# Down projection by block products over pairs of chunks, and products accumulated onto one another in PSUM

## The chip, the cores and the metric

The kernel runs on one core of a Trainium2 chip. The metric is device time in microseconds (us) of one execution; smaller is better. Engines are named as the profile names them: PE is TensorE (matmul), DVE is VectorE, ACT is ScalarE, POOL is GpSimd, SP is SyncE, which issues most loads and stores.

## What is computed

One layer of a hybrid decoder on 1024 tokens of width 1024: a token mixer (linear attention and sliding-window attention) and a gated MLP with a causal convolution of three taps. The change touches the MLP alone:

```
h2 = rms_norm(x, ffn_norm)
u = causal_dwconv(h2 @ w_up, conv_w, conv_b)     # w_up: 1024 x 5632
a, bval = jnp.split(u, 2, axis=-1)               # 2 x 2816
return x + (jax.nn.silu(a) * bval) @ w_down      # w_down: 2816 x 1024
```

All of it is float32. A float32 operand is split into a high half (`CAST` on ACT) and a low half (a subtraction, `split`), and a product is three matmul passes: high by high, high by low, low by high (`PASSES`).

## The kernel before

The hidden width of 2816 is cut into 22 chunks of 128 (`NCH`). A chunk takes 128 columns of the a side and 128 of the b side of `w_up`, for all 1024 tokens in two halves of 512.

**Up projection.** In chunks 1 to 20 the 2 by 2 blocks (side by token half, and 1024 rows of `w_up` in two halves) are made with seven block products instead of eight, the Strassen-Winograd scheme. `up_operand` builds the sums S1 to S4 on POOL, casts the high half on ACT and subtracts the low half on POOL; the token side (T1 to T4) is built once, in `norm2_sums`. Each of P1 to P7 is 12 matmuls of 128x512 into a PSUM bank of its own (`bank`, a pool of eight), and `post` adds the products up in SBUF: P1 and P5 are copied by ACT, DVE adds the other five, and from chunk 2 on POOL makes two more additions. `conv` is one ACT instruction (last tap and bias) and two DVE instructions (`tap`) on each half; `conv_edge` carries two columns from one token half to the other. `silu` is on ACT, `glu` multiplies a and b on DVE and splits the result into `g` (high half ACT, low half DVE). Chunks 0 and 21 use eight plain products (R1, R2, X1 to X4).

**Down projection.** For each chunk, 16 times (8 token tiles by 2 column halves), `down` makes three matmuls into a bank and DVE adds the bank to the SBUF accumulator `acc` (five of chunk 20's go over ACT and POOL, `VIA_POOL`). The down work of chunk c stands between the products of chunk c+1, as `SEQ` says: so many after each product.

**What sets the order.** All work is put into a list of events with a time each (`at_us`), sorted, and issued in that order; a scheduler of the framework then moves single instructions within each engine's queue. An engine's queue is executed in order. Operands are prepared four products ahead (`LAG`); the split operands lie in slots of SBUF (`SLOTS`: seven for the up side, two for the down side).

Of the kernel before, what the change touches and what calls it, by code (L numbers as in the profile page):

```python
# [35 lines left out]
def hymba_layer_kernel(ctx, tc, x, mix_norm, w_in, w_alpha2, b_alpha, gla_norm,  # L36
# [31 lines left out]
    SLOTS = {"w": tuple(i % 9 for i in range(48)) + (9, 3, 4, 5, 6, 7, 8, 0),  # L68
             "u": (1, 2, 3, 4, 5, 6, 7), "d": (8, 0)}
    used = {"w": 0, "u": 0, "d": 0}  # L70

    def w_tile(name, kind="w"):
        slots = SLOTS[kind]
        slot = slots[used[kind] % len(slots)]
        used[kind] += 1
        p = w_late["pool"] if slot == 9 else w_keep
        return p.tile([P, 2, 512], F32R, tag=f"w{slot}", name=name, bufs=1)
# [631 lines left out]
    def b_operand(name, k, r):  # L709
# [9 lines left out]
            "X3": ("A21", "T1"), "X4": ("A22", "B22")}  # L719

    def product(ch, name, part=None):
        an, bn = PROD[name]
# [1 line left out]
        first, last = name not in ("X2", "X4"), name not in ("X1", "X3")
        key = {"X1": "X2", "X3": "X4"}.get(name, name)
        if first and not part:
            psb[key, ch] = bank(f"{key}_{ch}")
        pb = psb[key, ch]
# [38 lines left out]
    done = {ch: set() for ch in range(NCH)}

    def post(ch, name):
        eng = dve if ch < 2 else pool  # L770

        def early(n):
            if ch:
                return half_tile(f"{n}_{ch}")
            if n in ("P1c", "R1c"):
                psb["early", n] = w_tile(f"{n}_0", "d").bitcast(F32)
            return psb["early", {"c11": "P1c", "c21": "R1c"}.get(n, n)][:, int(n[0] == "c")]

        if name in ("X1", "X3"):
            return  # L780
        pb = psb.pop((name, ch))
        if name in ("P1", "P5", "R1"):
            p = psb[name.lower(), ch] = early(f"{name}c")
            act.copy(p, pb)
        elif name == "P6":
            u2 = psb["u2", ch] = half_tile(f"u2_{ch}")
            dve.tensor_add(u2, psb["p1", ch], pb)
        elif name == "P2":
            c11 = psb["p1", ch] if "P6" in done[ch] else early("c11")
            dve.tensor_add(c11, psb["p1", ch], pb)  # L790
            conv(ch, 0, 0, c11, None)
# [255 lines left out]
```

## Time and profile before

| | us |
|---|---|
| median of 3 runs (1126.53 to 1126.87) | 1126.79 |
| the profiled execution, its own time | 1127.78 |
| its span, first to last instruction | 1125.9 |
| PE busy in the span | 1103.6 |
| POOL busy | 617.4 |
| DVE busy | 809.0 |
| ACT busy | 443.7 |

Busy time is the time in which an engine has an instruction in execution. DVE and POOL instructions that stand in each other's way show as longer instructions, not as idle time. A "releaser" is the engine and line whose result ended a wait. Matmuls overlap: one takes 0.40 us from start to end, and twelve in a row 2.80 us. MLP times in the trace: chunk 1 begins at 451 us, chunk 2 at 483 us, and the last chunks end with the span.

### The profile page before, as it was taken

Reading aid. Unit: us, or ns where it says so; the run is one execution under the profiler, and the core shown is the slowest. Engines: PE = TensorE matmul, PEld = TensorE weight load, DVE = VectorE, ACT = ScalarE, POOL = GpSimd, SP = SyncE. Lnnn points to the kernel's source line nnn. Section 1 sums busy time; section 2 is a strip of 40 time slices with the busy share of each in tenths; the row PEclk is TensorE's granted clock in tenths of the full one; section 3 lists DMA queues with packets and bytes.
Section 4 is the critical chain, followed back from the end, with each engine's and each line's share of the span. In section 5 each row is a group of like instructions: output and inputs, shape, how many; then the busy total and the mean of one; then the engine's idle time right before and its main releaser. Section 6 shows DMA issues by size and latency. Waiting matters only on the chain.

```text
span 1125.9 us, 14419 instructions
## 1 busy us (share of the span) xinstructions
PE 1103.6 (98%) x5276; PEld 887.4 (79%) x5276; DVE 809.0 (72%) x1479; ACT 443.7 (39%) x889; POOL 617.4 (55%) x491
## 2 busy tenths in 40 slices
PE   7999999999999999989999999999999999999997
PEld 5897778777888877778888888888888888888885
DVE  6646557766231489998878777777988788787777
ACT  5326655434240354433333433343434343333322
POOL 5356323334450356867657667776666666667402
PEclk9999999999999999999999999999999999999999
DMA  6124123002034101211111111111111211111103
GB/s 207 49 74 125 41 57 75 20 1 77 1 102 160 57 1 38 60 54 56 56 56 56 57 38 38 57 56 56 47 48 56 57 57 57 56 32 45 56 1 149
DMA packets 67344, 67.16 MB, mean 60 GB/s; under 512 B 4616, under 2 KB 51913, under 8 KB 67274
## 3 DMA queue, kind: packets, MB, share of 16 engines
q1 hardware_dynamic: 63432, 61.53, 17.7%
q10 hardware_dynamic: 3842, 4.73, 1.8%
q8 instruction: 41, 0.67, 0.2%
q14 instruction: 29, 0.24, 0.1%
HBM read 57.33 MB, written 4.19 MB: 55 GB/s over the span
## 4 chain that ended last, share of the span: by engine, by line
PE 87%; DVE 7%; POOL 3%; ACT 1%; issue 1%; DMA 1%; SPq 0%; POOLq 0%; DVEq 0%; ACTq 0%
PE P L734 33%; PE dn L852 20%; PE do L283 5%; PE dg L283 4%; PE dr L283 4%; PE dv L283 4%; PE dq L283 3%; PE dk L283 2%; DVE cu L755 2%; PE pv L444 1%; PE dq L633 1%; PE ppt L432 1%; PE X L734 1%; PE go L547 1%; PE go L543 1%
## 5 line engine op out<-in xcount | busy, mean ns | idle before, releaser
L852 PE MATMUL dn<-dnw,g 128*128 128x512 f32 x1056 | 270.1, 399 | 6.4 <-DVE g L836 3.0
L852 PEld LDWEIGHTS dn<-dnw,g 128*128 128x128 f32 x1056 | 199.9, 190 | 56.4 <-DVE g L836 3.4
L861 DVE TENSOR_TENSOR acc<-acc,dn 128x512 f32<-128x512 f32 x347 | 227.8, 681 | 2.7 <-PE dn L852 1.2
L283 PE MATMUL do<-wow,big 128*128 128x512 f32 x384 | 91.5, 397 | 0.0
L283 PEld LDWEIGHTS do<-wow,big 128*128 128x128 f32 x384 | 71.5, 188 | 16.8
L755 DVE SCALAR_TENSOR_TENSOR cu<-u,cc,cu 128x511 f32<-128x511 f32 (+2 forms) x120 | 80.4, 695 | 0.0
L84 POOL TENSOR_TENSOR dnw<-dn,dnw 128x512 fp32r<-128x512 f32 x44 | 57.5, 1307 | 28.9 <-ACT dnw L81 28.9
L84 POOL TENSOR_TENSOR A22w<-up,A22w 128x512 fp32r<-128x512 f32 x22 | 29.5, 1342 | 69.8 <-ACT A22w L81 65.7
L755 DVE SCALAR_TENSOR_TENSOR cu<-P1c,cc,cu 128x511 f32<-128x511 f32 (+1 forms) x46 | 51.1, 1110 | 21.5 <-ACT cu L747 21.3
L734 PE MATMUL P<-big,A11w 128*128 128x512 f32 x264 | 65.6, 396 | 0.9 <-ACT big L244 0.9
L421 POOL TENSOR_TENSOR pr<-pr,sm 128x1024 f32<-128x1024 f32 (+1 forms) x16 | 28.6, 1787 | 66.9 <-DVE sm L419 51.2
L734 PE MATMUL P<-big,A12w 128*128 128x512 f32 x264 | 65.3, 396 | 0.0
L734 PE MATMUL P<-big,S1w 128*128 128x512 f32 x240 | 62.4, 395 | 0.0
L734 PEld LDWEIGHTS P<-big,A11w 128*128 128x128 f32 x264 | 49.4, 188 | 13.1 <-ACT big L244 1.1
L734 PE MATMUL P<-ex,S2w 128*128 128x512 f32 x240 | 59.2, 395 | 0.0
L734 PE MATMUL P<-ex,S3w 128*128 128x512 f32 x240 | 59.2, 395 | 0.0
L734 PE MATMUL P<-ex,A22w 128*128 128x512 f32 x240 | 59.1, 395 | 0.0
L734 PE MATMUL P<-big,S4w 128*128 128x512 f32 x240 | 59.1, 395 | 0.0
L734 PEld LDWEIGHTS P<-big,A12w 128*128 128x128 f32 x264 | 49.6, 188 | 11.8
L836 DVE TENSOR_TENSOR g<-cu,g 128x512 fp32r<-128x512 f32 (+1 forms) x46 | 47.2, 1031 | 15.4 <-ACT g L835 15.4
L765 ACT ACTIVATE cu<-cu 128x512 f32<-128x512 f32 x44 | 27.9, 633 | 73.6 <-DVE cu L755 73.5
L734 PEld LDWEIGHTS P<-big,S1w 128*128 128x128 f32 x240 | 45.4, 189 | 11.0
(403 smaller groups left out, 2318.4 us busy)
## 6 DMA issues: line engine op xcount, KB each, us to landing
up<-in_w_up_dram SPq DMA_DIRECT2D x44, 512.0 KB, 3.8
dn<-in_w_down_dram SPq DMA_DIRECT2D x22, 512.0 KB, 4.2
acc<-in_x_dram SPq DMA_DIRECT2D x8, 512.0 KB, 7.9
out_dram<-acc SPq DMA_DIRECT2D x16, 256.0 KB, 2.1
xt<-in_x_dram SPq DMA_DIRECT2D x7, 512.0 KB, 4.4
qraw<-in_w_in_dram SPq DMA_DIRECT2D x4, 512.0 KB, 7.6
vraw<-in_w_in_dram SPq DMA_DIRECT2D x4, 512.0 KB, 3.5
qt<-qt ACTq DMA_DIRECT2D x16, 128.0 KB, 2.3
```

What stands on the lines that cost most here:

```text
L84: (eng or pool).tensor_sub(lo, src, hi.bitcast(F32))
L283: pe.matmul(pb[:, :n], lhsT=big[:, t, k, ra, :], rhs=ws[k][:, rb, :n], start=(k == 0 and i == 0), stop=(k == KD - 1 and i == 2))
L421: pool.tensor_tensor(pr[:, :, s0:], pr[:, :, s0:], den[:, hs].rearrange("p (j o) -> p j o", o=1).broadcast_to((P, 4, n)), ALU.mult)
L432: pe.transpose(pb[:, j * P:(j + 1) * P], pr[:, j, b * P:(b + 1) * P], ident)
L444: pe.matmul(pb[g * 64:(g + 1) * 64, :], lhsT=vv[:, t - 1 + b, g * 64:(g + 1) * 64], rhs=pts[t, g][:, b, :], start=(b == b0), stop=(b == 1))
L543: pe.matmul(pb[:, h * P:(h + 1) * P], lhsT=a[:, lo, pr * P:(pr + 1) * P], rhs=v[:, h * P:(h + 1) * P], start=(h == 0), stop=False)
L734: pe.matmul(pb[:, ts.start * P:ts.stop * P], lhsT=w[:, ra, k, :], rhs=b_operand(bn, k, rb)[:, ts], start=(first and i == 0), stop=(last an ...
L755: dve.scalar_tensor_tensor(dst, src, w, dst, op0=ALU.mult, op1=ALU.add)
L765: act.activation(u, u, AF.Silu)
L836: dve.tensor_sub(gt[:, 1], ub, gt[:, 0].bitcast(F32))
L852: pe.matmul(pb, lhsT=g[:, ra, (t % 4) * P:(t % 4 + 1) * P], rhs=w[:, rb, :], start=(i == 0), stop=(i == 2))
L861: dve.tensor_add(acc[:, cs], acc[:, cs], pb)
```

## The change

**Down projection.** Chunks 0 to 19 are taken in ten pairs. The 2 by 2 blocks (chunk of the pair by token half, and chunk by column half) are made with seven block products. A unit `down_pair(p, k, j)` is product k of pair p for two token tiles: six matmuls (2 tiles by 3 passes) into a pair of banks, one bank for each tile, and one DVE addition of 128x2x512 from both banks to `acc`. A product is two units, so a pair has 14 units. `down_w` makes the weight side (four POOL combinations in a pair, seven splits on ACT and POOL), `down_g` the token side (four DVE combinations, seven splits on ACT and DVE). One unit stands after each up product, from the second product of chunk 2 to the first of chunk 20, then two. Chunks 20 and 21 stay plain (`down_row`).

**Accumulation in PSUM.** P6, P7 and P4 are accumulated onto P1's bank and P3 onto P5's (`ONTO`), after the earlier content has been read; the down products likewise (`ONTO_DOWN`): P6, P7 and P4 onto P1's banks, P3 onto P5's. `post` so loses two DVE additions of a chunk and both POOL additions; the taps of P4 read PSUM. P2 now stands ahead of P6 in `SEQ`.

**Storage.** PSUM is four single banks for the up products and two pairs of banks for the down units (`open_banks`). The up operands have three slots in turn and are prepared two products ahead instead of four; the combinations are written over the loaded weights. The down operands have two slots on each side, and the rows of `w_down` two. `VIA_POOL` goes; `silu` of a chunk is one instruction over 1024 columns.

```diff
+NPAIR = NCH // 2 - 1
-VIA_POOL = ((NCH - 2, 3, 1), (NCH - 2, 4, 1), (NCH - 2, 5, 1), (NCH - 2, 6, 1), (NCH - 2, 7, 1))
...
+    def open_banks():
+        ps_first.close()
+        ps["b"] = ctx.enter_context(tc.tile_pool(name="psu", bufs=4, space=PSUM))
+        ps["d"] = ctx.enter_context(tc.tile_pool(name="psd", bufs=2, space=PSUM))
...
         if name == "S2":
-            s1 = combo("S1", "tensor_add", a21, a22)
-            src = combo("S2", "tensor_sub", s1, a11)
+            s1 = psb["S1", ch] = fin["ff"].tile([P, 4, P], F32, tag="s", name=f"S1_{ch}", bufs=1)
+            pool.tensor_add(s1, a21, a22)
+            pool.tensor_sub(a21, a11, a21)
+            pool.tensor_sub(a11, s1, a11)
...
+            slot = 1 + turn[0] % 3
...
+    ONTO = {"P6": "P1", "P7": "P1", "P4": "P1", "P3": "P5"}
...
     def post(ch, name):
...
+        if name == "P1":
+            ca = psb["ca", ch] = wide_tile(f"ca{ch}", "ca")
+            act.copy(ca[:, 0:512], pb)
+        elif name == "P2":
+            ca = psb["ca", ch]
+            dve.tensor_add(ca[:, 0:512], ca[:, 0:512], pb)
+            ua = psb["ua", ch] = wide_tile(f"ua{ch}", "ua")
+            conv(ch, 0, ua, ca, 0, 512, True)
         elif name == "P6":
+            act.copy(psb["ca", ch][:, 512:], pb)
+        elif name == "P5":
+            p5 = psb["p5", ch] = half_tile(f"p5_{ch}")
+            act.copy(p5, pb)
         elif name == "P7":
+            p5 = psb["p5", ch]
+            dve.tensor_add(p5, p5, pb)
+            ub = psb["c", ch, 1] = half_tile(f"ub1_{ch}")
+            conv(ch, 1, ub, p5, 0, 512, True)
+        elif name == "P3":
+            ca, ua = psb["ca", ch], psb["ua", ch]
+            dve.tensor_add(ca[:, 512:], ca[:, 512:], pb)
+            conv(ch, 0, ua, ca, 512, 1024, False)
+            silu(ua)
         elif name == "P4":
+            ub = psb["c", ch, 0] = half_tile(f"ub0_{ch}")
+            conv(ch, 1, ub, pb, 0, 512, True)
+            conv_edge(ch, 1, psb["c", ch, 1], pb[:, 510:512])
             glu(ch, 0)
             glu(ch, 1)
...
+    DOWN = (("P1", 0, 0), ("P6", 0, 1), ("P7", 1, 1), ("P4", 1, 0), ("P5", 1, 1), ("P3", 0, 1), ("P2", 0, 0))
+    ONTO_DOWN = {"P6": "P1", "P7": "P1", "P4": "P1", "P3": "P5"}
...
+    def down_w(p, k):
...
+        if k == 1:
+            t2 = psb["T2", p] = fin["ff"].tile([P, 512], F32, tag="t2", name=f"T2_{p}", bufs=1)
+            pool.tensor_sub(b11, b12, b11)
+            pool.tensor_sub(t2, b22, b11)
+            pool.tensor_sub(b12, b22, b12)
+        if k == 3:
+            pool.tensor_sub(psb["T2", p], b21, psb["T2", p])
...
+        w = blocks["d", p, k] = slot_tile(4 + (7 * p + k) % 2, f"dw{p}_{k}")
+        split(src, w[:, 0], w[:, 1])
+
+    def down_g(p, k):
...
+        if k == 1:
+            s1, s2 = psb["D1", p], psb["D2", p] = half_tile(f"D1_{p}"), half_tile(f"D2_{p}")
+            dve.tensor_add(s1, a21, a22)
+            dve.tensor_sub(s2, s1, a11)
+            dve.tensor_sub(a21, a11, a21)
+        if k == 5:
+            dve.tensor_sub(psb["D2", p], a12, psb["D2", p])
...
+        g = blocks["g", p, k] = slot_tile(6 + (7 * p + k) % 2, f"dg{p}_{k}")
+        split(src, g[:, 0], g[:, 1], dve)
+
+    def down_pair(p, k, j):
+        name, th, nh = DOWN[k]
+        onto = ONTO_DOWN.get(name)
+        if onto is None:
+            psb["d", p, name, j] = two_banks(f"dn{p}_{name}_{j}")
+        pb = psb["d", p, onto or name, j]
+        g, w = blocks["g", p, k], blocks["d", p, k]
+        for i in range(2):
+            for n, (ra, rb) in enumerate(PASSES):
+                c = (2 * j + i) * P
+                pe.matmul(pb[:, i], lhsT=g[:, ra, c:c + P], rhs=w[:, rb, :],
+                          start=(onto is None and n == 0), stop=(n == 2), skip_group_check=onto is not None)
+        t = 4 * th + 2 * j
+        acc = fin["all"][:, t:t + 2, nh * 512:(nh + 1) * 512]
+        dve.tensor_add(acc, acc, pb)
...
-    SEQ = (("P1", 0), ("P6", 0), ("P2", 3), ("P5", 3), ("P7", 4), ("P3", 3), ("P4", 3))
+    SEQ = ("P1", "P2", "P6", "P5", "P7", "P3", "P4")
...
-            at_us(max(1.9 + 0.01 * n, prods[n - LAG][2]), up_operand, ch, op)
+            at_us(max(1.9 + 0.01 * n, prods[n - 2][2] + 0.01), up_operand, ch, op)
```

The change moves instructions in every queue of the MLP. Three places matter for what follows.

PE in the middle of the MLP. Before: chunk 10, from P7 to P4; `dn9_6_0` is the down work of chunk 9 for token tile 6 and column half 0.

```order
L734 MATMUL P7_10_6846<-ex_3519,S3w_10_6743 128x512 x12
L852 MATMUL dn9_6_0_6876<-dnw9_0_6696,g9_1_6710 128x512 x3
L852 MATMUL dn9_7_0_6881<-dnw9_0_6696,g9_1_6710 128x512 x3
L852 MATMUL dn9_0_1_6886<-dnw9_1_6746,g9_0_6706 128x512 x3
L852 MATMUL dn9_1_1_6891<-dnw9_1_6746,g9_0_6706 128x512 x3
L734 MATMUL P3_10_6896<-big_62,S4w_10_6765 128x512 x12
```

The changed kernel: chunk 8 from P2 to P7. `dn3_P1_0` is the bank pair of pair 3 for j = 0, first written by product P1 (operands `dw3_0`, `dg3_0`) and then by P6 (`dw3_1`, `dg3_1`).

```order
L749 MATMUL P2_8_5927<-big_62,A12w_8_5872 128x512 x12
L904 MATMUL dn3_P1_0_5963<-dw3_0_5875,dg3_0_5878 128x512 x6
L749 MATMUL P1_8_5897<-ex_3512,S2w_8_5914 128x512 x12
L904 MATMUL dn3_P1_1_5987<-dw3_0_5875,dg3_0_5878 128x512 x6
L749 MATMUL P5_8_5995<-big_62,S1w_8_5940 128x512 x12
L904 MATMUL dn3_P1_0_5963<-dw3_1_5947,dg3_1_5955 128x512 x6
L749 MATMUL P1_8_5897<-ex_3512,S3w_8_5983 128x512 x12
L904 MATMUL dn3_P1_1_5987<-dw3_1_5947,dg3_1_5955 128x512 x6
```

One unit of six matmuls stands after each up product, and the same bank pair returns two units later.

DVE after P4 of a chunk. Before: chunk 9.

```order
L755 SCALAR_TENSOR_TENSOR cu9_1_0_6700<-u3_9_6613,cc_140,cu9_1_0_6700 128x510
L834 TENSOR_TENSOR cu9_1_1_6617<-cu9_0_1_6658,cu9_1_1_6617 128x512
L834 TENSOR_TENSOR cu9_1_0_6700<-cu9_0_0_6536,cu9_1_0_6700 128x512
L836 TENSOR_TENSOR g9_0_6706<-cu9_1_0_6700,g9_0_6706 128x512
L787 TENSOR_TENSOR u2_10_6768<-P1c_10_6749,P6_10_6751 128x512
L836 TENSOR_TENSOR g9_1_6710<-cu9_1_1_6617,g9_1_6710 128x512
```

The changed kernel: chunk 7, the second of pair 3, from the second product of a and b (L780) on; `D1` and `D2` are the combinations of `down_g`.

```order
L780 TENSOR_TENSOR ub1_7_5820<-ua7_5723,ub1_7_5820 128x512
L885 TENSOR_TENSOR D1_3_5950<-ub1_6_5596,ub1_7_5820 128x512
L908 TENSOR_TENSOR acc_3440<-acc_3440,dn2_P2_1_5919 128x2x512
L886 TENSOR_TENSOR D2_3_5951<-D1_3_5950,ub0_6_5656 128x512
L887 TENSOR_TENSOR ub1_6_5596<-ub0_6_5656,ub1_6_5596 128x512
L789 TENSOR_TENSOR ca8_5917<-ca8_5917,P2_8_5927 128x512
L87 TENSOR_TENSOR dg3_1_5955<-D2_3_5951,dg3_1_5955 128x512
L908 TENSOR_TENSOR acc_3440<-acc_3440,dn3_P1_0_5963 128x2x512
L889 TENSOR_TENSOR D2_3_5951<-ub0_7_5881,D2_3_5951 128x512
L757 SCALAR_TENSOR_TENSOR ua8_5959<-ca8_5917,cc_140,ua8_5959 128x511
L757 SCALAR_TENSOR_TENSOR ua8_5959<-ca8_5917,cc_140,ua8_5959 128x510
L908 TENSOR_TENSOR acc_3440<-acc_3440,dn3_P1_1_5987 128x2x512
```

Combinations and the low half of the second operand now stand ahead of the addition that empties `dn3_P1_0`, and a combination and two taps ahead of the one that empties `dn3_P1_1`.

ACT in chunk 1. Before, the copies of P1 and P5 (L784):

```order
L765 ACTIVATE cu0_0_1_4400<-cu0_0_1_4400 128x512
L784 COPY P1c_1_4454<-P1_1_4434 128x512
L81 CAST dnw0_1_4451<-dn0_4366 128x512
L81 CAST A11w_2_4531<-up2_0_4491 128x512
L835 CAST g0_1_4427<-cu0_1_1_4417 128x256 x2
L81 CAST A12w_2_4614<-up2_0_4491 128x512
L747 ACTIVATE cu1_0_0_4496<-P1c_1_4454,cc_140 128x512
```

The changed kernel; L793 is the copy of P6, which shares P1's bank:

```order
L776 ACTIVATE ua0_4355<-ua0_4355 128x512
L786 COPY ca1_4410<-P1_1_4390 128x512
L84 CAST dg0_0_4494<-ub0_0_4362 128x512
L84 CAST S4w_1_4465<-up1_0_4351 128x512
L84 CAST A22w_1_4484<-up1_1_4353 128x512
L762 ACTIVATE ua1_4429<-ca1_4410,cc_140 128x512
L793 COPY ca1_4410<-P1_1_4390 128x512
L796 COPY p5_1_4470<-P5_1_4451 128x512
```

P6's copy, which empties the bank for P7, stands behind the convolution on P2's sum.

## Rows read from the trace of the kernel before

**Rows 1.** The page: span, and busy time of PE.

```profile
span 1125.9 us, 14419 instructions
PE 1103.6 (98%) x5276; PEld 887.4 (79%) x5276; DVE 809.0 (72%) x1479; ACT 443.7 (39%) x889; POOL 617.4 (55%) x491
```

**Rows 2.** Waits of PE: who waited for whom; us in total, times, longest.

```profile
PE dn L852 <- DVE g L836: 3.0, 1, 3.0
PE dn L852 <- ACT g L835: 2.9, 1, 2.9
```

**Rows 3.** The chain that ended last, 579 to 611: start us, us, what.

```profile
580.14 8.40 PE P L734 x36
588.53 1.41 PE dn L852 x6
...
610.90 0.23 PE P L734
```

**Rows 4.** Busy time of each engine, 580 to 1070 (instructions), then the granted clock.

```profile
580.00:1070.00 490.00, 490.00 (x2104) 394.93 (x2103) 395.40 (x604) 184.57 (x302) 329.55 (x236) 1.00 0.18 52
```

**Rows 5.** DVE groups by form, 580 to 1065: busy us, mean ns, idle before.

```profile
L861 DVE TENSOR_TENSOR acc<-acc,dn 128x512 f32<-128x512 f32 x252 | 165.8, 682 | 1.5 <-PE dn L852 0.5
L836 DVE TENSOR_TENSOR g<-cu,g 128x512 fp32r<-128x512 f32 x32 | 35.1, 1098 | 11.0 <-ACT g L835 11.0
L755 DVE SCALAR_TENSOR_TENSOR cu<-u,cc,cu 128x511 f32<-128x511 f32 x31 | 35.0, 1129 | 0.0
...
L755 DVE SCALAR_TENSOR_TENSOR cu<-u,cc,cu 128x510 f32<-128x510 f32 x31 | 23.0, 741 | 0.0
...
L798 DVE TENSOR_TENSOR u<-u,P 128x512 f32<-128x512 f32 x16 | 11.0, 686 | 23.7 <-PE P L734 23.7
...
L755 DVE SCALAR_TENSOR_TENSOR cu<-u,cc,cu 128x2 f32<-128x2 f32 x16 | 3.3, 207 | 0.0
```

**Rows 6.** DVE, whole run: a tap-like instruction with one input from PSUM.

```profile
L572 DVE SCALAR_TENSOR_TENSOR big<-ogt,glan,big 128x512 fp32r<-128x512 f32 x8 | 6.0, 748 | 30.8 <-ACT big L571 30.8
```

**Rows 7.** POOL groups by form, 580 to 1065.

```profile
L84 POOL TENSOR_TENSOR dnw<-dn,dnw 128x512 fp32r<-128x512 f32 x33 | 42.5, 1289 | 15.8 <-ACT dnw L81 15.8
L84 POOL TENSOR_TENSOR A11w<-up,A11w 128x512 fp32r<-128x512 f32 x16 | 27.9, 1745 | 2.0 <-ACT A11w L81 2.0
...
L84 POOL TENSOR_TENSOR A22w<-up,A22w 128x512 fp32r<-128x512 f32 x17 | 22.1, 1302 | 61.7 <-ACT A22w L81 57.6 <-PE dn L852 4.1
```

**Rows 8.** DVE in order of time around 707: start us, us, what.

```profile
706.48 1.28 DVE L834 TENSOR_TENSOR cu<-cu,cu 128x512 f32<-128x512 f32 x2
708.45 1.02 DVE L836 TENSOR_TENSOR g<-cu,g 128x512 fp32r<-128x512 f32 x1 [0.69 <-ACT g L835]
```

**Rows 9.** POOL in order of time around 707.

```profile
707.08 1.84 POOL L691 TENSOR_TENSOR S<-up 128x512 f32<-128x512 f32 x1 [1.86 <-DMA up<-in_w_up_dram]
708.88 1.75 POOL L84 TENSOR_TENSOR A11w<-up,A11w 128x512 fp32r<-128x512 f32 x1
```

**Rows 10.** ACT groups by form, 580 to 1065.

```profile
L747 ACT ACTIVATE cu<-u,cc 128x512 f32<-128x512 f32 x31 | 25.2, 811 | 0.0
...
L784 ACT COPY P1c<-P 128x512 f32<-128x512 f32 x16 | 9.4, 587 | 34.9 <-PE P L734 34.9
```

**Rows 11.** PE in order of time: start of chunk 1, and two waits.

```profile
451.20 2.97 PE L734 MATMUL P<-big,A11w 128*128 128x512 f32 x12
...
494.44 2.93 PE L852 MATMUL dn<-dnw,g 128*128 128x512 f32 x6 [2.86 <-ACT g L835]
...
1114.61 7.41 PE L852 MATMUL dn<-dnw,g 128*128 128x512 f32 x24 [2.95 <-DVE g L836]
```

**Rows 12.** PE busy, granted clock (1 is full) and DMA right after that wait.

```profile
494.40:497.20 2.80, 2.76 (x7) 0.50 0.00 0
```

**Rows 13.** DVE in order of time: chunk 0, and the last chunk.

```profile
449.64 1.59 DVE L834 TENSOR_TENSOR cu<-cu,cu 128x512 f32<-128x512 f32 x1
...
1106.09 0.75 DVE L824 TENSOR_TENSOR R1c<-R1c,X 128x256 f32<-128x256 f32 x2 [3.65 <-PE X L734]
...
1114.13 0.42 DVE L836 TENSOR_TENSOR g<-cu,g 128x256 fp32r<-128x256 f32 x1
```

More of the change, by code (lines that the diff above doesn't have):

```diff
@@ L67, in hymba_layer_kernel, with slot_tile, w_tile @@
     idp = swp.enter_context(tc.tile_pool(name="idp", bufs=1, side="right"))
[L68 to L77, printed above, removed]
+    SLOTS = tuple(i % 9 for i in range(48)) + (9, 3, 4, 5, 6, 7, 8, 0)
+    used = [0]
+    def slot_tile(slot, name, dt=F32R):
+        return w_keep.tile([P, 2, 512], dt, tag=f"w{slot}", name=name, bufs=1)
+    def w_tile(name):
+        slot = SLOTS[used[0]]
+        used[0] += 1
+        if slot == 9:
+            return w_late["pool"].tile([P, 2, 512], F32R, tag="w9", name=name, bufs=1)
+        return slot_tile(slot, name)
     def split(src, hi, lo, eng=None, hi_eng=None):
@@ L588, in open_acc @@
         fp = ctx.enter_context(tc.tile_pool(name="fp", bufs=1))
-        fin["acc"] = [fp.tile([P, D], F32, name=f"acc{t}") for t in range(NT)]
+        acc = fin["all"] = fp.tile([P, NT, D], F32, name="acc")
+        fin["acc"] = [acc[:, t, :] for t in range(NT)]
     def open_norm2():
@@ L723, in product @@
         w = blocks["u", ch, an]
[L724 to L728, printed above, removed]
+        onto = (ONTO_PLAIN if ch in PLAIN else ONTO).get(name)
+        if onto is None and not part:
+            psb[name, ch] = bank(f"{name}_{ch}")
+        pb = psb[name, ch] = psb[onto or name, ch]
         ts = slice(0, 4) if part is None else slice(2 * part, 2 * part + 2)
@@ L735, in product, with tap @@
                       rhs=b_operand(bn, k, rb)[:, ts],
-                      start=(first and i == 0), stop=(last and i == 11))
+                      start=(onto is None and i == 0), stop=(i == 11), skip_group_check=onto is not None)
     def half_tile(name):
-        return fin["ff"].tile([P, 512], F32, tag="h", name=name, bufs=7)
-    def conv(ch, sd, hf, y, edge, a=0, z=512):
+        return fin["ff"].tile([P, 512], F32, tag="h", name=name, bufs=9)
+    def tap(dst, src, w):
+        dve.scalar_tensor_tensor(dst, src, w, dst, op0=ALU.mult, op1=ALU.add)
@@ L765, in silu, with glu @@
+    def silu(u):
         act.activation(u, u, AF.Silu)
[L767 removed]
+    def glu(ch, hf, a=0, z=512):
+        ub = psb["c", ch, hf][:, a:z]
+        dve.tensor_mul(ub, psb["ua", ch][:, hf * 512 + a:hf * 512 + z], ub)
     def post(ch, name):
[L770 to L784, printed above, removed]
[L785 to L806 removed]
@@ new lines, in down_row @@
+    def down_row(ch, t):
+        pb = two_banks(f"dn{ch}_{t}")
+        g = gtiles[ch, t // 4]
+        acc = fin["all"][:, t]
+        last = ch == NCH - 1
+        for hf in range(2):
+            w = blocks["d", ch, hf]
+            for i, (ra, rb) in enumerate(PASSES[::-1] if last else PASSES):
+                pe.matmul(pb[:, hf], lhsT=g[:, ra, (t % 4) * P:(t % 4 + 1) * P], rhs=w[:, rb, :],
+                          start=(i == 0), stop=(i == 2))
+            if last:
+                cs = slice(hf * 512, hf * 512 + 512)
+                dve.tensor_add(acc[:, cs], acc[:, cs], pb[:, hf])
+                sp.dma_start(out[t * P:(t + 1) * P, cs], acc[:, cs])
+        if not last:
+            dve.tensor_add(acc, acc, pb.rearrange("p h n -> p (h n)"))
```

265 lines of the change are left out of this document (148 added, 117 removed).

## The prediction

> **What bounds the kernel now.** I read the page first, then PE's waits, then the chain, then each engine's load in the MLP. PE is busy for 1103.6 of 1125.9 us [rows 1] and waits 2.9 to 3.0 us at two places of the MLP [rows 2]. In its middle the chain is PE alone: one chunk lasts from 580.14 to 610.90, 30.77 us, for 7 x 12 + 16 x 3 = 132 matmuls, 0.233 us each [rows 3]; a product takes 2.80 us, six matmuls 1.40. So a matmul less is 0.233 us less as long as PE still finds its operands and its banks. The reader should then see how near the others are. From 580 to 1070, when PE is busy all the time, DVE is busy for 395.4 of 490 us and POOL for 329.6 [rows 4]: in two chunks (61.5 us) DVE 49.6, POOL 41.4. And they hold each other up. Two DVE instructions with both inputs in SBUF take 0.64 each while POOL rests [rows 8], the same kind 1.10 or 1.13 on average where POOL works [rows 5]; DVE instructions fed by PSUM stay at 0.68 [rows 5]. The place where this is seen is 708: POOL's instruction ends at 707.08 + 1.84 = 708.92, DVE's low half of g, begun at 708.45, ends 0.55 later at 709.47, and POOL's next, begun at 708.88, ends 1.16 later at 710.63 [rows 8, 9]. They take turns, a whole instruction each.
>
> **PE's gain.** A pair of chunks costs 2 x 132 = 264 matmuls now and 2 x 84 + 14 x 6 = 252 afterwards: 12 less, 2.80 us, so 58.8 us instead of 61.5 for a pair, and 28.0 us less for ten. That the up products share banks takes no matmul away.
>
> **DVE's load** hardly falls. A pair then has 14 wide additions, 6 narrow ones, 4 taps and 8 edges fed by PSUM, and 27 instructions with both inputs in SBUF (call these S): 12 taps, 4 products of a and b, 7 low halves, 4 combinations; now there are 24 S. No row has a wide addition; between 128x2 at 0.21 and 128x512 at 0.68 [rows 5] a line gives 1.16 for 1024 columns, an estimate. A tap fed by PSUM is 0.75 [rows 6]. Then 14 x 1.16 + 6 x 0.69 + 4 x 0.75 + 8 x 0.21 = 25.1, and 27 S at 0.93, the middle of their means of 0.74 and 1.13 [rows 5], are 25.1: 50.2 of 58.8 us, 85% instead of 81%. **POOL** has 33 instructions for a pair instead of 30 (two additions fewer in each chunk; three splits and four combinations more in the pair): at the present 41.4 / 30 = 1.38 each, 45.5 us, 77%. The turns alone, 33 x 1.16 + 27 x 0.55, are 53.1 of 58.8 us. So no engine is overloaded and PE's beat can hold; but nothing has much room, and POOL's long rests (3.6 us in a chunk ahead of A22w [rows 7], where DVE now runs its taps undisturbed) go.
>
> The Trainium skill, page "SBUF — State Buffer", section "Who interferes with whom", says that a DVE instruction contends with POOL only if it has two SBUF inputs, and that the later one waits for the whole instruction. The trace agrees with the second part, as shown; for taps fed by PSUM no row has POOL busy beside them. If they did contend, a pair would have 31 S and the place below two more, some 1 us more stall for each pair.
>
> **Where PE can stall.** The tight place is the second chunk of each pair. P6 of the down projection (k = 1) goes onto the banks of P1, so its units wait until DVE has added P1's unit to `acc`; and its operand needs D1 and D2, hence both chunks' results. From the end of that chunk's up P7 to the second unit of k = 1, PE has 7 x (2.80 + 1.40) = 29.4 us of other work. In DVE's queue there stand in this time six wide additions (7.0), three narrow (2.1), two taps (1.5) and two edges (0.4) fed by PSUM, and 14 S, which alone take 14 x 0.64 = 9.0: 19.9 us, and 0.7 us in which DVE must wait for a unit. That leaves 8.8 us, 0.63 for each S to wait for POOL. Bounds: at the present excess, 0.93 - 0.64 = 0.29 each, 4.1 us are used and PE does not stall. If POOL is always ready, the eight S that directly follow another wait 1.07 (a turn of 1.16 + 0.55, less 0.64) and the other six half of that: 11.8 us, a stall of 3.0. I take 2.0, nearer the upper end: at this place POOL has the next chunk's combinations, A11, A12, S2 and four instructions of `down_w` standing ready one behind the other, as in the row pair at 707, where they alternate [rows 8, 9]. Eight pairs (1 to 8): +16 us, between 0 and 24. A stall of this size is in two pieces, and the clock need not fall.
>
> **The start.** In chunk 1 no down work is left between the products. P7 goes onto P1's bank and waits for ACT's copy of P6; that stands behind the convolution of P2's sum, which waits for DVE's add, which stands behind 11 S of chunk 0 from 449.6 on [rows 13]. 11 x 0.64 to 11 x 1.71 and two additions (1.4), then 0.81 + 0.59 on ACT [rows 10], give 459.4 to 471.2; P7 is due at 451.2 + 4 x 2.8 = 462.4 [rows 11]. A stall of 0 to 9, taken as 4; another 2 for pair 0. After a wait of 2.86 the granted clock stood at 0.50, 1.2 GHz, and six matmuls took 2.93 instead of 1.57 [rows 11, 12], so 1.4 more. Saved are today's stall of 2.86 and its 1.4. Sum +3, between -4 and +8.
>
> **The end.** Two units follow each product in chunk 20, so the second unit of k = 1 comes 5.6 us earlier: with 2.0 a stall of 7.6. Saved is the last stall, 2.95 and about 1.8 of half-speed matmuls after it: PE then has six rows, 8.4 us, beside a chain of DVE that now takes 1106.1 to 1114.6 with POOL in the way [rows 11, 13]. Sum +3, between -5 and +8.
>
> **Costed at nothing:** POOL's operands for PE (each has 9.8 us from the freeing of its slot to its use, for an ACT cast and a POOL instruction of 1.3 to 1.7 [rows 7]; without that cover a lost product costs up to 2.8); ACT, which gets longer silus and six more casts in a pair; the loads, of the same bytes, one each 30 us.
>
> **Sum:** 1127.8 - 28.0 + 16 + 3 + 3 = 1121.8 for the profiled execution, which stands 1.0 above the median: 1121.
>
> **Rivals.**
> (1) The gain arrives whole. For it: the present excess of S is 0.29, under the 0.63 that is free; a rest of POOL at the right place is enough. Then no stalls, the end gives 3 back: 1127.8 - 28 - 3 - 1 = 1096 to 1106 with the start's stall and some. Against: the rests that give that excess are used up.
> (2) DVE becomes the bound, and the kernel slower. Mechanism: turns with POOL in the second chunk of each pair. It decides at a wait above 0.83 for each S there (28 - 6 = 22 us over eight pairs is 2.75 each; (8.8 + 2.75) / 14). At 11.8 us of waiting: 1127.8 - 28 + 24 + 8 + 8 - 1 = 1139. For it: DVE's queue is 85% full and ordered, and a late DVE holds `silu`, hence ACT's copies. The Trainium skill, page "SBUF — State Buffer", section "Who interferes with whom", says that the loser waits for the whole instruction, and the trace agrees [rows 8, 9]; where every S meets a ready POOL that gives this time.
> (3) ACT's copies are late: the copy of P1 must be done within 5.6 us of P1's end, and in ACT's queue it stands behind a silu that waits for DVE's taps. At 1 us a chunk this is 20 us more: 1141. Against: 5.6 us hold nine copies.
>
> **Numbers.** Forecast 0.43 (own range 1110 to 1132), rival 1 0.22, rival 2 0.28, rival 3 0.07. The range leaves out a tenth at each end: 1102 to 1140. A measurement can tell about 0.2%, that is 1124.5 to 1129.0, from no change. Faster: rival 1 and seven tenths of the forecast, 0.52; same: two tenths of it and a little of rival 2, 0.12; slower 0.36.
>
> **What would show it.** Right: in the middle of the MLP a pair takes about 60.8 us; PE's waits are new and lie at the units of k = 1, released by the wide addition (L908) or a low half (L87); S instructions on DVE average above 1.0; POOL's idle share falls. Rival 1: 58.8 us for a pair and no such waits. Rival 2: 61.6 or more. Rival 3: PE's waits are released by ACT copies (L786, L793). The forecast is wrong if the waits lie at up products for their operands, if the wide addition takes far from 1.16, or if the clock falls at every pair.

## The result, and the profile after

The change made the kernel a little slower: 1129.09 us (median of 9 runs, 1128.37 to 1131.93) against 1126.53 (9 runs), a ratio of 1.0035 with an interval of 1.0021 to 1.0048. The forecast was 1121, faster. The time lies inside the range of 1102 to 1140, but on the other side of no change.

The page of the changed kernel: span, and busy time of each engine. It answers to [rows 1].

```profile
span 1128.5 us, 14126 instructions
PE 1080.7 (96%) x5156; PEld 860.6 (76%) x5156; DVE 865.9 (77%) x1251; ACT 478.0 (42%) x946; POOL 689.9 (61%) x518
```

PE works 22.9 us less than before, and the span is 2.6 longer. PE's waits, from 430 us on (who waited for whom; us in total, times, longest), answer to [rows 2]:

```profile
PE dn_P L904 <- DVE acc L908: 14.4, 10, 2.0
PE P L749 <- DVE ub L757: 9.5, 1, 9.5
PE dn_P L904 <- ACT dw L84: 5.7, 8, 0.8
...
PE dn L933 <- DVE acc L940: 1.4, 4, 0.6
PE dn_P L904 <- ACT ca L793: 1.2, 1, 1.2
```

Where the time went can be read from the starts of the chunks on PE. "Lost" is the length less 0.233 us for each matmul of the stretch; the last row has some 3.9 us behind the last matmul in either kernel.

| stretch | before, us | after, us | matmuls before, after | lost before | lost after |
|---|---|---|---|---|---|
| up to chunk 1 | 451.2 | 449.3 | the same | | |
| chunks 1 to 3 | 98.0 | 89.1 | 396, 330 | 5.7 | 12.2 |
| chunks 4 to 19 (8 pairs) | 492.3 | 491.4 | 2112, 2016 | 0.2 | 21.7 |
| chunk 20 to the end | 84.4 | 98.6 | 324, 366 | 8.9 | 13.3 |

120 matmuls fewer are 28.0 us, as forecast. 32.4 us of new waiting stand against them; the forecast had 22. The 1.9 us of the first row are a gain too, for which the forecast had no term: nearly all of them lie in chunk 0, whose order on PE the change alters as well. From the first matmul of chunk 0 to the first of chunk 1 PE takes 25.6 us before and 23.8 after; the runs below show 23.8 too, but for no_pool_low (24.5) and the two with the banks dealt out ahead of chunk 1. Before, eight small matmuls waited there for DVE:

```profile
433.18 1.29 PE L208 MATMUL n2pt<-ident,n2h 128*128 128x128 f32 x8 [1.50 <-DVE n2h L198]
```

In the changed kernel a product (A12w, from 431.42 on) stands ahead of them, and the wait is gone.

**The middle.** PE in order of time, chunk 8 (start us, us, what, and the wait ahead of it). The other seven pairs have the same two waits (one of the first is 0.26 only):

```profile
734.94 2.96 PE L749 MATMUL P<-big,S1w 128*128 128x512 f32 x12
738.69 1.62 PE L904 MATMUL dn_P<-dw,dg 128*128 128x512 f32 x6 [0.79 <-ACT dw L84]
740.15 2.97 PE L749 MATMUL P<-ex,S3w 128*128 128x512 f32 x12
744.65 1.64 PE L904 MATMUL dn_P<-dw,dg 128*128 128x512 f32 x6 [1.53 <-DVE acc L908]
```

These are the two units of k = 1. With some 0.2 us of restart each they cost 2.7 us: a pair takes 61.4 us instead of 58.7. The name on the first wait misleads. What ended just ahead of 738.69 is DVE's wide addition, 737.34 + 1.21 = 738.55; the cast named was of an operand that PE needs later. (In the program this unit waits for that addition, for the cast of its own operand `dg3_1`, which ended at 734.68, and for POOL's half of `dw3_1`.) In all nine waits that are put down to ACT here (eight to L84, one of 1.2 us to L793) a wide addition ended 0.15 us before PE went on. DVE's queue over the same time:

```profile
715.34 3.52 DVE L757 SCALAR_TENSOR_TENSOR ub<-p,cc,ub 128x511 f32<-128x511 f32 x2
...
727.21 1.67 DVE L780 TENSOR_TENSOR ub<-ua,ub 128x512 f32<-128x512 f32 x1
...
732.21 1.21 DVE L908 TENSOR_TENSOR acc<-acc,dn_P 128x1024 f32<-128x1024 f32 x1
733.34 0.68 DVE L886 TENSOR_TENSOR D<-D,ub 128x512 f32<-128x512 f32 x1
733.95 1.78 DVE L887 TENSOR_TENSOR ub<-ub,ub 128x512 f32<-128x512 f32 x1
735.65 0.68 DVE L789 TENSOR_TENSOR ca<-ca,P 128x512 f32<-128x512 f32 x1
736.25 1.17 DVE L87 TENSOR_TENSOR dg<-D,dg 128x512 fp32r<-128x512 f32 x1
737.34 1.21 DVE L908 TENSOR_TENSOR acc<-acc,dn_P 128x1024 f32<-128x1024 f32 x1
738.47 1.61 DVE L889 TENSOR_TENSOR D<-ub,D 128x512 f32<-128x512 f32 x1
740.00 3.47 DVE L757 SCALAR_TENSOR_TENSOR ua<-ca,cc,ua 128x511 f32<-128x511 f32 x2
743.39 1.21 DVE L908 TENSOR_TENSOR acc<-acc,dn_P 128x1024 f32<-128x1024 f32 x1
```

The additions at 737.34 and 743.39 are the ones that PE waits for. Ahead of the first stands L887, a combination that the third operand needs; ahead of the second L889, for the sixth operand. From 714.9 to 744.6 DVE is busy for 29.4 of 29.7 us, POOL for 26.6. The 14 S (DVE instructions with both inputs in SBUF) in that time take 21.1 us, 1.51 each.

Busy time from 570 to 1000 (PE, PEld, DVE, ACT, POOL with instructions, then the granted clock) and two groups of DVE in the same stretch answer to [rows 4 to 6]:

```profile
570.00:1000.00 430.00, 414.44 (x1766) 330.05 (x1765) 400.77 (x386) 188.37 (x309) 352.80 (x231) 1.00 0.17 52
```

```profile
L908 DVE TENSOR_TENSOR acc<-acc,dn_P 128x1024 f32<-128x1024 f32 x98 | 118.7, 1211 | 24.8 <-PE dn_P L904 24.7
...
L757 DVE SCALAR_TENSOR_TENSOR ub<-P,cc,ub 128x511 f32<-128x511 f32 x14 | 10.4, 741 | 0.0
```

DVE is busy for 93% of this time and POOL for 82%. The 190 S there (their groups added up) take 251 us, 1.32 each.

### The profile page after: what moved, and what is told of

The parts are those of the page before. It is cut to its first block, busy times and chain, and to the rows that moved or that the text cites. A ratio compares the mean times of both kernels' runs of the same rounds, so it can differ in the third digit from the quotient of the medians.

```text
span 1128.5 us, 14126 instructions
## 1 busy us (share of the span) xinstructions
PE 1080.7 (96%) x5156; PEld 860.6 (76%) x5156; DVE 865.9 (77%) x1251; ACT 478.0 (42%) x946; POOL 689.9 (61%) x518
## 4 chain that ended last, share of the span: by engine, by line
PE 67%; DVE 27%; issue 2%; ACT 2%; DMA 1%; POOL 0%; SPq 0%; ACTq 0%; POOLq 0%
PE P L749 20%; PE dn_P L904 11%; PE do L286 5%; DVE ub L757 4%; DVE ua L757 4%; PE dg L286 4%; PE dr L286 4%; DVE acc L908 4%; PE dv L286 4%; PE dq L286 3%; DVE ub L780 3%; DVE dg L87 2%; PE X L749 2%; PE dk L286 2%; DVE ub L887 1%
## 5 line engine op out<-in xcount | busy, mean ns | idle before, releaser
L904 PE MATMUL dn_P<-dw,dg 128*128 128x512 f32 x840 | 217.8, 394 | 21.3 <-DVE acc L908 14.4
L904 PEld LDWEIGHTS dn_P<-dw,dg 128*128 128x128 f32 x840 | 155.7, 188 | 65.3 <-DVE acc L908 19.9
L908 DVE TENSOR_TENSOR acc<-acc,dn_P 128x1024 f32<-128x1024 f32 x140 | 169.5, 1211 | 41.2 <-PE dn_P L904 41.0
L757 DVE SCALAR_TENSOR_TENSOR ua<-ca,cc,ua 128x511 f32<-128x511 f32 (+1 forms) x80 | 95.9, 1199 | 2.7 <-ACT ua L762 1.8
L87 POOL TENSOR_TENSOR dw<-dn,dw 128x512 fp32r<-128x512 f32 x50 | 82.9, 1658 | 19.4 <-ACT dw L84 19.4
L749 PE MATMUL P<-big,A11w 128*128 128x512 f32 x264 | 68.0, 406 | 10.4 <-DVE ub L757 9.5
L780 DVE TENSOR_TENSOR ub<-ua,ub 128x512 f32<-128x512 f32 (+1 forms) x45 | 63.1, 1402 | 0.8
L757 DVE SCALAR_TENSOR_TENSOR ub<-p,cc,ub 128x511 f32<-128x511 f32 (+1 forms) x40 | 57.2, 1431 | 4.5 <-ACT ub L762 4.1
L749 PE MATMUL P<-ex,S3w 128*128 128x512 f32 x240 | 59.6, 397 | 0.2 <-ACT ca L793 0.2
L749 PE MATMUL P<-big,S4w 128*128 128x512 f32 x240 | 59.6, 396 | 0.0
L762 ACT ACTIVATE ua<-ca,cc 128x512 f32<-128x512 f32 x40 | 32.7, 818 | 62.9 <-DVE ca L804 44.2
L749 PEld LDWEIGHTS P<-big,A12w 128*128 128x128 f32 x264 | 49.6, 188 | 11.8 <-ACT early L821 0.2
L87 DVE TENSOR_TENSOR dg<-ub,dg 128x512 fp32r<-128x512 f32 x40 | 54.3, 1357 | 2.4 <-ACT dg L84 0.5
L749 PEld LDWEIGHTS P<-ex,S3w 128*128 128x128 f32 x240 | 45.0, 188 | 11.4 <-ACT ca L793 0.6
```

Source lines behind the costliest of these rows:

```text
L87: (eng or pool).tensor_sub(lo, src, hi.bitcast(F32))
L757: dve.scalar_tensor_tensor(dst, src, w, dst, op0=ALU.mult, op1=ALU.add)
L780: dve.tensor_mul(ub, psb["ua", ch][:, hf * 512 + a:hf * 512 + z], ub)
L904: pe.matmul(pb[:, i], lhsT=g[:, ra, c:c + P], rhs=w[:, rb, :], start=(onto is None and n == 0), stop=(n == 2), skip_group_check=onto is no ...
L908: dve.tensor_add(acc, acc, pb)
```

## The experiments

**1. Two combinations behind the additions (late_combos).** In the changed kernel the program issues the first of them (L887) early, together with those for k = 1; the second (L889) it issues with k = 5, and the scheduler moved it forward.

```diff
-            dve.tensor_sub(a21, a11, a21)
+        if k == 2:
+            with tc.issue_after(accs[p, 0, 1]):
+                dve.tensor_sub(a21, a11, a21)
         if k == 5:
-            dve.tensor_sub(psb["D2", p], a12, psb["D2", p])
+            with tc.issue_after(accs[p, 0, 1]):
+                dve.tensor_sub(psb["D2", p], a12, psb["D2", p])
```

> Two of the four combinations of the token side (a21 - a11 for the third operand, D2 for the sixth) are queued on DVE behind the wide addition of unit (k = 0, j = 1) instead of ahead of it. Theory 1 (the order of DVE's queue): in the changed kernel 1.7 us of S stand ahead of the first addition that PE waits for and 3.3 ahead of the second; with them behind, the two waits of each pair (0.77 and 1.52 us at 738 and 744) are gone, a pair takes 58.8 to 59.3 us instead of 61.4, and the time falls by 16 to 21 us, to 1108 to 1113. DVE is then busy for 57.2 of 59 us. Theory 2 (DVE as a whole is full, 57.2 us of work in a pair with POOL in its way): the waits move to later units of the same chunk (k = 1 or 2), a pair stays at 60.5 or more, the time at 1122 or more.

Measured: 1103.24 us, ratio 0.9805 (0.9786 to 0.9823). The same stretch of 570 to 1000, and DVE at the place:

```profile
570.00:1000.00 430.00, 430.00 (x1847) 346.85 (x1847) 408.75 (x404) 198.75 (x324) 370.34 (x241) 1.00 0.18 55
```

```profile
731.70 1.21 DVE L913 TENSOR_TENSOR acc<-acc,dn_P 128x1024 f32<-128x1024 f32 x1
732.84 0.68 DVE L889 TENSOR_TENSOR ub<-ub,ub 128x512 f32<-128x512 f32 x1
733.44 0.68 DVE L892 TENSOR_TENSOR D<-ub,D 128x512 f32<-128x512 f32 x1
734.20 0.69 DVE L87 TENSOR_TENSOR dg<-ub,dg 128x512 fp32r<-128x512 f32 x1
```

PE is busy for all of the 430 us, a pair takes 58.72, eight pairs gain 21.7. The rest, 4.1 us, came at the end (chunk 20 to the end now 94.6 instead of 98.6): pair 9 has the same place. The expectation had left that out, so the time is below its 1108 to 1113. DVE is busier than ever, 95%, and PE does not wait for it; the S still take 1.27 us on average (249.5 us for 197). So the order was it, and not DVE's whole load. Both combinations now take 0.68 where they took 1.78 and 1.61, since POOL rests just then:

```profile
735.25 1.30 POOL L87 TENSOR_TENSOR A22w<-up,A22w 128x512 fp32r<-128x512 f32 x1 [2.31 <-ACT A22w L84]
```

**2. One of the two (one_late).** L889 behind the addition, L887 left ahead.

> The changed kernel with one of the two combinations queued behind the wide addition (that of D2 for the sixth operand, 1.6 us); the other (1.8 us) stays ahead of both additions. Theory (each microsecond of S ahead of an addition is a microsecond of wait): the first wait of a pair (0.77) stays, the second (1.52) goes; a pair takes 60.0 to 60.3 us instead of 61.4 (0.77 and some 0.2 to 0.5 of restart remain), and the end gains 1 to 2 us: 1129.1 - 8 x 1.4 - 1.5 = 1116, 1113 to 1119. Rival (a threshold: PE waits as long as any S too many is there, or DVE has caught up altogether): within 2 us of 1129, or down to late_combos' 1103.

Measured: 1115.42 us, ratio 0.9894 (0.9877 to 0.9912), as expected; a pair takes 59.6 us, a little under the expected 60.0 to 60.3. Of PE's two waits the first remains, in every pair (0.26 to 0.78 us):

```profile
732.75 1.62 PE L907 MATMUL dn_P<-dw,dg 128*128 128x512 f32 x6 [0.78 <-ACT dw L84]
```

Each combination is worth its own place in the queue; the rival, a threshold, did not come.

**3. POOL with 14 instructions fewer in a pair (no_pool_low).** The high halves stand where the low halves of the up operands were.

```diff
-        split(src, w[:, 0], w[:, 1])
+        act.copy(w[:, 0], src)
```

> The low halves of the up operands of chunks 1 to 20 are not made and the high half stands in their place in the same matmuls: POOL has 19 instructions in a pair instead of 33, DVE, ACT, PE and their order keep theirs. Theory 1 (DVE instructions with two SBUF inputs take turns with POOL): the mean S on DVE falls from 1.32 us (570 to 1000) to about 1.0 and DVE's load from 57.2 to about 48 us a pair; the waits at k = 1 shrink to under 0.5 us a pair or go, a pair takes 58.8 to 59.3, the time 1106 to 1113. Theory 2 (the S are long for another cause): S stays above 1.25, the waits stay above 2 us a pair, the time within 4 us of the changed kernel's.

Measured: 1103.24 us, ratio 0.9802 (0.9788 to 0.9817), with DVE's order as in the changed kernel.

```profile
570.00:1000.00 430.00, 430.00 (x1847) 346.88 (x1846) 363.67 (x399) 197.51 (x320) 197.71 (x138) 1.00 0.19 56
```

POOL is at 46% instead of 82%, the mean S falls from 1.32 to 1.04 us (203.3 us for 196), and the waits are gone, from 61.4 to 58.72 for a pair; the time is below the expected 1106 to 1113. So the length of S comes from POOL, and either cure is enough: fewer turns, or an order in which the turns don't stand ahead of what PE needs.

**4. Without accumulation for the up products (no_up_accum).** Products in banks of their own, DVE adding P6 and P4 in SBUF, POOL making two additions a chunk.

```diff
-        onto = (ONTO_PLAIN if ch in PLAIN else ONTO).get(name)
+        onto = (ONTO_PLAIN if ch in PLAIN else {}).get(name)
```

> One part of the change undone: P6, P7, P4 and P3 of the up projection go into banks of their own; DVE adds P6 and P4 in SBUF and POOL makes two additions a chunk, as before the change; the block products of the down projection stay. Theory 1 (DVE and its turns with POOL are the limit of the changed kernel): a pair has 4 more additions fed by PSUM on DVE (2.7 us), 4 taps that become S (2.4 us or more) and 4 more POOL instructions (6 us), so DVE has 62 us or more of work in a pair and PE follows it: 62 to 66 us a pair, the time 1135 to 1170. Theory 2 (the accumulation only saves work that lies beside PE's): the time within 4 us of the changed kernel's.

Measured: 1207.24 us, ratio 1.0724 (1.0702 to 1.0745), a pair 69.8 us (the last of the eight 72.8): far more than either figure. A group of DVE from 570 to 1000, and PE's first row of waits:

```profile
L808 DVE TENSOR_TENSOR ca<-ca,P 128x512 f32<-128x512 f32 x13 | 8.9, 688 | 43.3 <-POOL ca L802 43.3
```

```profile
PE dn_P L910 <- DVE acc L914: 57.1, 26, 4.3
```

I had costed only load. What came besides is a dependence: DVE's addition of P3 waits for a POOL addition, 3.3 us in each chunk, with everything queued behind it on DVE, wide additions too. And behind some of PE's waits of 2.9 us and more its next six matmuls took up to 2.93 us instead of 1.6, the granted clock being 0.97 on the mean. So without the accumulation in PSUM the block products of `down` do not pay, at least in this order of DVE's queue (the two combinations stood ahead here too); the accumulation takes POOL out of DVE's chain.

**5. The last rows in single banks (end_banks).**

```diff
-        pb = two_banks(f"dn{ch}_{t}")
+        pb = None if last else two_banks(f"dn{ch}_{t}")
         for hf in range(2):
+            pbh = bank(f"dn{ch}_{t}_{hf}") if last else pb[:, hf]
```

> The rows of the last chunk go into single banks of the up products' four (one for each column half) instead of pairs of banks shared with chunk 20's rows. Theory 1: the last rows advance at 1.745 us a row instead of 1.40 since each next row waits for DVE to empty the only other pair; with eight banks for them the last 45 matmuls go at 0.233 us instead of 0.293, PE's waits for L940 (1.4 us) go, and the time falls by 3 to 6 us. Theory 2: DVE is what the rows wait for anyhow (1.39 us of additions for 1.40 of matmuls), and the time falls by less than 1.5 us.

Measured: 1124.79 us, ratio to before 0.9996 (0.9985 to 1.0008), 4.3 us less than the changed kernel. DVE in the changed kernel, and then PE in this one:

```profile
1119.32 1.39 DVE L937 TENSOR_TENSOR acc<-acc,dn 128x512 f32<-128x512 f32 x2 [0.35 <-PE dn L933]
1121.07 1.38 DVE L937 TENSOR_TENSOR acc<-acc,dn 128x512 f32<-128x512 f32 x2 [0.36 <-PE dn L933]
```

```profile
1096.89 19.49 PE L934 MATMUL dn<-dnw,g 128*128 128x512 f32 x84
```

In the changed kernel a row took 1.745 us, with DVE waiting for PE and PE for DVE by turns: the program queues the column halves of two rows crosswise (row 0, row 1, row 0, row 1), so both pairs of banks are held until the second half is added, and three matmuls begin only when the addition two places earlier has ended. With four single banks beside the two pairs 84 matmuls go in one run at 0.232 us.

**6. Both gains together (late_end).**

> The two edits that gained, together: late_combos (two combinations behind the wide addition) and end_banks (the last chunk's rows in single banks). They lie at different places, so by both theories the gains should add: 1103.2 - 4.3 = 1099; if the last rows were only waiting for the same DVE queue that late_combos has already relieved, under 1.5 us are added, 1102.

Measured: 1098.59 us, ratio 0.9759 (0.9744 to 0.9773). The gains add; chunk 20 to the end takes 89.4 us, 84.9 of them up to the end of the last matmul and 4.5 behind it.

**7. The start: slot (start_slot).**

```diff
-                                             (6, 7, 8, 1, 2, 3, 7))})
+                                             (6, 7, 4, 1, 2, 3, 7))})
```

> One number: the operand S2w of chunk 1 lies in slot 4 instead of slot 8, so that the first rows of w_down need not wait for P6 to free slot 8. Theory 1: in the changed kernel this load lands at 466.9, the cast of it holds ACT for 5.07 us, and behind the cast stands the convolution that DVE and then PE wait for; without it the wait of 9.53 us ahead of chunk 2 falls to 4 to 6 us, and the time by 3.5 to 6 us. Theory 2 (the start is DVE's backlog of chunk 0 and its turns with POOL): the wait stays above 8.5, the time within 1.5 us.

Measured: 1128.96 us, ratio 1.0030, no gain, and the wait ahead of chunk 2 is still 9.5: the numbers of theory 2. ACT in chunk 1, first in the changed kernel, then here:

```profile
466.93 0.62 ACT L84 CAST dw<-dn 128x512 fp32r<-128x512 f32 x1 [5.07 <-DMA dn<-in_w_down_dram]
467.46 0.61 ACT L84 CAST A12w<-up 128x512 fp32r<-128x512 f32 x1
467.98 0.81 ACT L762 ACTIVATE ub<-p,cc 128x512 f32<-128x512 f32 x1
```

```profile
471.01 0.62 ACT L84 CAST S2w<-up 128x512 fp32r<-128x512 f32 x1 [5.65 <-POOL up L708]
471.53 0.81 ACT L762 ACTIVATE ua<-ca,cc 128x512 f32<-128x512 f32 x1
```

The load came in time, and the next cast in ACT's queue waited instead, again with a convolution behind it. So this run does not decide between theory 2 and one more unready cast; the next run moves both casts away.

**8. The start: ACT's order (le_act).** late_end with the slot of 7 and two casts behind the last convolution of chunk 1.

```diff
+        if (ch, name) == (2, "S2"):
+            with tc.issue_after(convs[1]):
+                split(src, w[:, 0], w[:, 1])
```

> late_end, the slot of start_slot, and the casts of S2w of chunk 2 and of the second operand of w_down queued on ACT behind the last convolution of chunk 1. start_slot showed that the wait for the load (5.07 us) was taken over by a wait of ACT for POOL's combination (5.65 us) with the convolution of P3's sum queued behind. Theory 1 (whatever stands unready ahead of the convolutions on ACT holds DVE and so PE): DVE's idle times at 459 to 472 go, the wait of 9.5 us falls to 5 to 7.5, the time by 2 to 4.5 us against late_end. Theory 2 (POOL's turns with DVE set the start): less than 1 us.

Measured: 1097.33 us against late_end's 1098.59; chunks 1 to 3 take 88.2 us instead of 89.8, PE's wait ahead of chunk 2 8.1 instead of 9.8. That is 1.3 us, between the two theories. The wait now ended with this chain on DVE, its last edge tap behind a product that waits for the silu.

```profile
473.55 1.35 DVE L786 TENSOR_TENSOR ub<-ua,ub 128x512 f32<-128x512 f32 x1 [1.20 <-ACT ua L782]
474.83 0.21 DVE L761 SCALAR_TENSOR_TENSOR ub<-P,cc,ub 128x2 f32<-128x2 f32 x1
```

**9. The start: the edge first (le_edge).** le_act, with chunk 1's two products of a and b queued behind that edge.

> le_act, and in chunk 1 the two products of a and b queued on DVE behind the last edge of the convolution (128x2, 0.21 us), which reads the PSUM bank of P4. In le_act the wait of PE ahead of chunk 2 ended with this edge at 474.83, and ahead of it stood a wait of DVE for the silu (1.20) and a product (1.35). Theory: the wait falls by 2.4 us, from 8.1 to 5.7, and the time by 1.5 to 2.5 us against le_act, 1095. Rival: the units of pair 0 wait for their operand instead (the D2 chain is no earlier), under 0.7 us.

Measured: 1096.18 us, ratio 0.9724 (0.9709 to 0.9738), the fastest here; the wait is 5.8 us, chunks 1 to 3 take 85.9. In the medians this is 1.2 us less than le_act. But before ran at 1126.23 beside le_act and at 1127.00 beside le_edge: by the ratios to it (0.9745, 0.9724) the gain is 2.4, and chunks 1 to 3 are 2.3 shorter, as expected.

**10. The start: banks (le_swap, le_open1, le_open1_edge).** le_swap exchanges the two lines of `open_banks`; le_open1 calls it ahead of chunk 1; the last adds the edit of 9.

> late_end with two lines exchanged: at the start of chunk 2 the pairs of banks for the down units are opened ahead of the single banks, so that they lie on other banks of PSUM; no instruction moves. Theory 1: the wait of 9.5 us ahead of chunk 2 comes from the bank alone (the first product of chunk 2 is given the bank that DVE's taps of chunk 1's P4 still read); on another bank PE goes on at once, the half clock after it (about 2 us) does not come, and later waits by the operands take part of it: 6 to 11 us less, 1088 to 1093. Theory 2: what is late is the work of chunk 1 itself (its taps and products, needed for the second operand at 483.7): the wait only moves to the units of pair 0, 0 to 3 us less.

> le_act, with the banks of PSUM dealt out anew ahead of chunk 1 instead of ahead of chunk 2. le_swap showed that the place of the banks does not matter, so what PE waits for at chunk 2 may be that the old banks are given back as a whole, the one of P4 of chunk 1 among them. Theory: then the wait of 8.1 us ahead of chunk 2 goes, and one of 2 to 5 us comes ahead of chunk 1, where DVE and ACT still read chunk 0's X4; the units of pair 0 wait 0 to 3 us for their operand: 2 to 6 us less than le_act, 1091 to 1095. Rival (the wait is for the operands or for P4's bank in any case): no gain or a loss, 1097 to 1101.

> le_open1 and le_edge together. If the bank is dealt out ahead of chunk 1, nothing waits for the last edge of chunk 1 at once, and the products of a and b come 0.2 us later: within 1 us of le_open1. If le_open1 does not take the wait away, le_edge's gain of 1.5 to 2.5 us comes on top.

Measured: 1097.77, 1098.14 and 1097.87 us. The exchange moved nothing (the wait is 9.9): whichever bank chunk 2's first product is given, it waits for DVE's last reading of the old ones. In the program of the changed kernel that product lies in bank 0 and waits for the last reading of P4 of chunk 1, which lies in bank 2, so the old banks are given back all together. With the banks dealt out ahead of chunk 1 the wait ahead of chunk 2 went, but the gain did not come. PE in le_open1:

```profile
453.25 4.52 PE L753 MATMUL P<-big,A11w 128*128 128x512 f32 x12 [3.68 <-DVE early L849]
...
490.66 2.08 PE L919 MATMUL dn_P<-dw,dg 128*128 128x512 f32 x4 [2.08 <-ACT dg L84]
492.95 3.78 PE L919 MATMUL dn_P<-dw,dg 128*128 128x512 f32 x8 [0.21 <-DVE dg L87]
```

There are two smaller waits in its place, the second for the operand made of D2, and behind each PE is slow for a while (twelve matmuls in 4.52 us instead of 2.97, the granted clock at 0.62 from 453.2 to 457.6 and at 0.50 from 490.6 to 496.6). The times are the rival's. That the chain of chunk 1 itself is the limit, about as long by either way, fits them; it is not shown apart.

## Why the prediction came out on the wrong side

**Right.** PE's gain, 28.0 us. The tight place, named to the unit: k = 1 in the chunk behind each pair, wide additions of DVE late behind S that take turns with POOL, in two pieces, with the clock at full (1.00 from 570 to 1000). A pair of 61.4 us lies between the forecast's 60.8 and rival 2's 61.6, nearer rival 2. Taps fed by PSUM were left open: they take 0.74 with POOL at 82%, so they don't contend. That is what the Trainium skill, page "SBUF — State Buffer", section "Who interferes with whom", says of DVE instructions with at most one SBUF input outside the two-port modes (the prediction left out this condition), and the trace agrees. PE's waits for ACT's copies (rival 3) did not come, but for 0.2 us.

**Wrong: the size of the stall of a pair.** The forecast took 2.0 us, with 10.8 us of waiting for 14 S, 0.77 each. Measured are 2.7, so this term is 21.6 instead of 16, the largest miss. The parts, in pair 3, are counted from the start of one DVE instruction to the start of the next, since the printed lengths overlap by some 0.08 us (732.21 + 1.21 against 733.34). The 14 S take 20.6, which is 11.6 of waiting, 0.83 each, just under the upper bound of 11.8. The instructions fed by PSUM take 10.4 instead of 11.0. That makes 2.3 of waiting, 0.79 + 1.53; the 0.4 of two restarts of PE had no term. The same kind of error is larger in the paragraph on DVE's load: 27 S at 0.93, a mean of the kernel before, where POOL was at 67%. Measured are 1.32, and DVE's load is 57.2 us a pair, not 50.2. There a mean over turns was carried to a place with more of them, though the alternation in [rows 8, 9] had been read correctly: 1.51 is nearly the 1.71 that it gives. With its upper bound for the stall, 24, the sum would have come to 1128.8; so close a hit would have been part luck, since it takes the other misses (-2.4, +3.5, +1.4 and -1.9) to cancel.

**Wrong: the start.** I looked for the stall at P7 of chunk 1, behind ACT's copy of P6. There it was 0.2 us. It was three products later, 9.5 us ahead of chunk 2, with about 2 more of slow matmuls: PE needs a bank, the old banks hang on DVE's last taps of chunk 1, and those hung on ACT, whose queue had a cast that was not ready ahead of two convolutions. Two steps failed. The change of the banks ahead of chunk 2 had no term, and "costed at nothing: ACT, the loads" was wrong: the cast of the first `w_down` rows waits for a load, and the load for the slot that P6 reads. Lost were 6.5 us more than before instead of 3. Of the wait, ACT's order is worth 1.7 us (9.8 to 8.1, experiment 8) and the place of the last edge 2.3 (experiment 9). Which part of the other 5.8 is turns with POOL stays open: no run took POOL alone out of the start (without the low halves the wait was 7.0).

**Wrong, but small: the end, and chunk 0.** The end lost 4.4 instead of 3. The stall of pair 9 cost 4.0, not 7.6, but the last rows, for which I had no term, cost as much (experiment 5). Chunk 0 gained 1.9, which was not forecast either.

The misses in the middle, at the start and at the end go one way, and 28 against 22 left no room for that: 28.0 + 1.9 against 32.4 is the other sign. Rival 2 gave this side as 1139, with the right mechanism in it, and the 0.83 for each S on which it was to decide is what pair 3 shows. What it had wrong is the word "bound": DVE at 95% and POOL at 86% do not hold PE up when the order is right (experiment 1).

## What to carry over

When a fast engine is given less work, look at what stands ahead of its releaser in the queue of the engine that it waits for, instruction by instruction, and ask of each whether it must stand there: here two subtractions, 0.68 us each when POOL rests, queued long before their use, cost 26 us of 1129. Price an instruction that contends at its worst turn if the other engine's queue is full, not at its mean in a kernel where that engine rests. And follow the first wait that you remove to the next one in the same queue before you expect a gain.

## What the runs showed of the hardware

- DVE instructions fed by PSUM keep their length: 0.74 us for a tap of 128x511 and 1.21 for an addition of 128x1024, with POOL at 82% and at 46% alike. The mean S went from 1.04 us (POOL at 46%) to 1.32 (82%), and to 1.51 in the 30 us where POOL was at 89%. The share is not all: it was 1.27 at 86% in late_combos, where two of the S fall into POOL's rests.
- A DVE instruction with two SBUF inputs can be held for the rest of POOL's, however short it is itself. In the changed kernel an edge of 128x1 with its inputs in SBUF, 0.20 us elsewhere, took 1.24: it ended at 452.46, POOL's split at 452.44.

```profile
451.22 1.24 DVE L757 SCALAR_TENSOR_TENSOR ua<-e,cc,ua 128x1 f32<-128x1 f32 x1
```

```profile
450.71 1.73 POOL L87 TENSOR_TENSOR S2w<-up,S2w 128x512 fp32r<-128x512 f32 x1
```

- PE's waits of 0.8 to 1.5 us, two in 61 us, left the granted clock at 1.00. Behind the 9.5 us wait twelve matmuls took 4.99 us instead of 2.97, with the clock at 0.72 from 480 to 486, a mean of its two levels: 0.50 (1.2 GHz) from 479.1 to 482, 1.00 (2.4 GHz) from 484 on. PE in order of time; then busy times and, behind them, the granted clock:

```profile
479.10 4.99 PE L749 MATMUL P<-big,A11w 128*128 128x512 f32 x12 [9.53 <-DVE ub L757]
```

```profile
480.00:486.00 6.00, 6.00 (x20) 4.71 (x19) 4.84 (x6) 1.73 (x3) 2.25 (x2) 0.72 0.00 0
```
